# The stick's sums as a rounded part and an exact rest, each multiplied in rounded float32

## The chip, the cores and the metric

The kernel runs on one core of a Trainium2 chip. Its time is device microseconds (us) of one execution. A core has five engines that work beside each other, each through its own queue in order: TensorE (PE: matrix products, with PEld for the loading of its stationary operand), VectorE (DVE), ScalarE (ACT), GpSimd (POOL) and SyncE (SP), which here only issues DMAs. PE writes into PSUM; the other data lies in SBUF.

## The reference, cut to what matters

Two layers over 2048 positions of width 1024. In each layer four groups of heads (A to D) mix the positions, are gated, and go through one output projection. The change lies in group A, stick-breaking attention with 4 heads of 64:

```python
z = einsum('bqhd,bshd->bhqs', qb, kk) * scale
log_1mb = where(strict, log_sigmoid(-z), 0.0)
between = reverse_cumsum(log_1mb) - log_1mb        # sums over later keys
a = where(strict, exp(log_sigmoid(z) + between), 0.0)
y = einsum('bhqs,bshd->bqhd', a, vv)
```

log_sigmoid(-z) is -softplus(z), and log_sigmoid(z) is z - softplus(z). So the exponent of a key is z minus the softplus of this key and of all later ones. That sum over keys is a product with a triangular matrix of minus ones inside a block of 128 keys, and with a full matrix of minus ones for the block after it.

## The kernel before, in words

A layer is a chain of sweeps in the order a, h, d0, d1, b, c, o. Each sweep has 16 steps, one per tile of 128 queries. Sweep a is the one in question: step i projects its tile (`a_prep`), makes the index scores of group C (`ci_prep`, `ci_turn`, `ci_score`), computes the stick's weights (`a_first`, L374) and multiplies them with the values (`a_second`, L425). From tile 4 on, searches for the 256th largest index score (`ci_search`, lines L528 to L656) run beside it: chains of very short DVE instructions on two columns, alternating with counts on ACT.

`a_first` looks at two blocks of keys only, the tile's own and the one before it (one block at i = 0), for 4 heads in two halves r = 0, 1. It goes: scores into the two PSUM tiles `tp` (L391), Abs (L396), Exp (L397) and Ln (L398) on ACT, which leave log(1+exp(-|z|)) in the SBUF tile `x4b`; then DVE adds max(z, 0) (L405), so that `x4b` holds the softplus, called sp here. PE then adds to `tp` the product of sp with `negU`, the triangle of minus ones (L409, 512 columns per half), and of the tile's own block with `nego`, all minus ones (L412, 256 columns per half). Exp (L414) turns `tp` into the weights in `x4c`, which `a_second` multiplies with the values (L436), copies (L440), transposes and writes to DRAM (L445, y<-o).

`negU`, `nego` and sp are float32. The other large products of this kernel (L267, L268, L271, L514, L515) take float32r operands, that is float32 rounded to the shorter form that PE multiplies in one pass, and get their accuracy by splitting a value into a rounded part and the rest (`split`, L199). The rest is made by `psub` (L191) on POOL.

The order of the instructions on each engine comes from two places. `drive` and `merge` weave the generators of a step by the costs that these yield, which sets a priority; a scheduler that simulates the program then orders each engine's queue by readiness and priority. A tile from a pool with `bufs` buffers waits for the last reader of the tile that had the buffer before: `x4b`, `x4c` have one buffer each, `o2` (L174, shown as `o`) has two and also holds `a_second`'s copy and its transposed result until the DMA y<-o has read it.

Of the kernel before, what the change touches and what calls it, by code (L numbers as in the profile page):

```python
# [10 lines left out]
F32 = mybir.dt.float32  # L11
F32R = mybir.dt.float32r
# [77 lines left out]
class Share:  # L90


    def __init__(self, g):
        self.g, self.tot, self.done = g, max(next(g), 1.0), 0.0
# [13 lines left out]
class Trunk:  # L108
    def __init__(self, ctx, tc, I, out, layers=2):
        self.tc, self.nc, self.I, self.out, self.layers = tc, tc.nc, I, out, layers  # L110
        nc = self.nc
        e = ctx.enter_context
        self.dram = e(tc.tile_pool(name="dram", bufs=1, space=DRAM))
        self.cst = e(tc.tile_pool(name="cst", bufs=1))
        self.wk = e(tc.tile_pool(name="wk", bufs=2))
        self.ps = e(tc.tile_pool(name="ps", bufs=2, space=PSUM))
        self.big = e(tc.tile_pool(name="big", bufs=1))
        self.ring = self.big.ring(R1)
        self.rows = self.big.ring(R2)
        dt = self.dram.tile  # L120
        self.hT = [dt([128, 2, KT, 128], F32, name=f"hT{i}") for i in range(NT)]
        self.y = [dt([128, D], F32, name=f"y{i}") for i in range(NT)]
        self.x1 = [dt([128, D], F32, name=f"x1_{i}") for i in range(NT)]
        self.gate = [dt([128, D], F32, name=f"gate{i}") for i in range(NT)]
        self.cT = [dt([128, 3, 128], F32, name=f"cT{i}") for i in range(NT)]
        self.kr = [dt([128, 32], F32, name=f"kr{i}") for i in range(NT)]
        self.sc = [dt([128, 128 * (i + 1)], F32, name=f"sc{i}") for i in range(NT)]
        self.out_of = [dt([128, S], I8, name=f"out_of{i}") for i in range(NT)]
        ct = self.cst.tile
        ld = nc.sync.dma_start  # L130
        self.ident = ct([128, 128], F32, name="ident")
        ld(self.ident, I["c_ident"])
        self.identr = ct([128, 128], F32R, name="identr")
        nc.scalar.copy(self.identr, self.ident)
        self.both = ct([128, 64], F32, name="both")
        self.identb = ct([128, 128], BF, name="identb")
        self.maskA = ct([128, 256], BF, name="maskA")
        self.maskR = ct([128, 512], BF, name="maskR")
        self.negU = ct([128, 128], F32, name="negU")
        self.nego = ct([128, 128], F32, name="nego")  # L140
        nc.gpsimd.memset(self.nego, -1.0)
        self.eps = ct([128, 1], F32, name="eps")
        nc.vector.memset(self.eps, EPS)
        self.mhalf = ct([128, 16], F32, name="mhalf")
        nc.gpsimd.memset(self.mhalf, -0.5)
        self.tie = ct([128, 256], F32, name="tie")
        self.iota9 = ct([128, 9], F32, name="iota9")
        self.junk = ct([128, S], I8, name="junk")
        self.chkA = ct([128, layers], F32, name="chkA")
        self.chkC = ct([128, layers, NT], F32, name="chkC")  # L150
        nc.vector.memset(self.chkC, float(TOPK))
        self.ev = 0

    def constants(self):

        I, ld = self.I, self.nc.sync.dma_start
        ld(self.identb, I["c_identb"])
        ld(self.maskA, I["c_maska"])
        ld(self.negU, I["c_negu"])
        ld(self.tie, I["c_tie"][None, :].to_broadcast([128, 256]))  # L160
        ld(self.iota9, I["c_iota9"])
        ld(self.both, I["c_both"])
        ld(self.maskR, I["c_maskr"])


    def g2(self, shape, dtype=F32):
# [207 lines left out]
    def a_first(self, l, i, st):  # L374
        nc = self.nc
        cur, prev = st["a", i], st.get(("a", i - 1))
        nb = 2 if prev else 1
        n = nb * 256
        yield 1740.0 + 220.0 + 2600.0
        z = [self.psum("tp", (128, 2, 2, 128)) for _ in range(2)]  # L380
        zf = [a.rearrange("p a b c -> p (a b c)") for a in z]
        t = cur[0]
        for r in range(2):
            nc.tensor.matmul(zf[r][:, :256], self.identb, self.maskA, start=True, stop=False, skip_group_check=True)
        yield 220.0
        for b in range(nb):
            kt = (cur, prev)[b][0]
            for p in range(2):
                for r in range(2):
                    q = slice(64 * r, 64 * r + 64)  # L390
                    nc.tensor.matmul(z[r][:, b, p, :], kt[q, 2 + p, :], t[q, p, :],  # L391
                                     start=False, stop=True, skip_group_check=True)
                yield 435.0
        sp = self.x4("b", [128, 2, 512])
        for r in range(2):
            nc.scalar.activation(sp[:, r, :n], zf[r][:, :n], AF.Abs)  # L396
        nc.scalar.activation(sp[:, :, :n], sp[:, :, :n], AF.Exp, scale=-1.0)  # L397
        nc.scalar.activation(sp[:, :, :n], sp[:, :, :n], AF.Ln, bias=1.0)  # L398
        zr = None
        if i >= 2:  # L400
            zr = self.wk.tile([128, 2, 256], F32, name="zr", bufs=1)[0:1]
            for r in range(2):
                nc.vector.tensor_copy(zr[:, r, :], zf[r][0:1, 256:])
        for r in range(2):
            nc.vector.scalar_tensor_tensor(sp[:, r, :n], zf[r][:, :n], 0.0, sp[:, r, :n], op0=OP.max, op1=OP.add)  # L405
        yield 0.0
        pt = self.x4("c", [128, 2, 512])
        for r in range(2):
            nc.tensor.matmul(zf[r][:, :n], self.negU, sp[:, r, :n], start=False, stop=(nb == 1), skip_group_check=True)  # L409
            yield 860.0  # L410
            if nb == 2:
                nc.tensor.matmul(zf[r][:, 256:], self.nego, sp[:, r, :256], start=False, stop=True,  # L412
                                 skip_group_check=True)
            nc.scalar.activation(pt[:, r, :n], zf[r][:, :n], AF.Exp)  # L414
            if zr is not None:

                nc.vector.scalar_tensor_tensor(zr[:, r, :], zr[:, r, :], -1.0, zf[r][0:1, 256:],
                                               op0=OP.mult, op1=OP.add)
            yield 430.0
        if zr is not None:  # L420
            ck = self.chkA[0:1, l:l + 1]
            nc.vector.tensor_scalar(zr, zr, 1.0, None if i == 2 else ck, op0=OP.mult, op1=OP.max, accum_out=ck)
        st["p", i] = pt
# [1049 lines left out]
```

## Time and profile before

| | |
|---|---|
| time, median of 3 runs | 4212.24 us (4211.06 to 4214.72) |
| the profiled execution's own time | 4215.46 us |
| its span, first to last instruction | 4213.2 us |
| PE, DVE, ACT, POOL busy | 93%, 66%, 55%, 32% of the span |
| mean granted clock of PE | 0.961 of full speed |
| sweep a of the two layers | about 12 to 407 us and 2131 to 2530 us |

Busy shares are means over the whole span; a share says what an engine did in a stretch, not who waited for whom. Matmuls overlap, so a matmul's printed duration is longer than the time that it keeps PE from the next one; that time is read from the distance of two starts. A row of the timeline can merge neighbours of one kind (x2: two instructions). One float32 product stands in the trace as two matmul instructions, a float32r product as one.

### The profile page before, as it was taken

How to read it: one execution, taken by the hardware profiler on the slowest of the kernel's cores; microseconds unless marked ns; L12 is line 12 of the kernel's file. 1: busy time of each engine (PE TensorE's matmuls, PEld its weight loads, DVE VectorE, ACT ScalarE, POOL GpSimd, SP SyncE). 2: the span in 40 equal slices, each digit the busy share in tenths (PEclk: the TensorE clock that was granted, in tenths of full speed). 3: DMA queues.
4: the chain of work that ended last, by engine and by line, in shares of the span. 5: the costliest groups of instructions: out<-in, count | busy, mean ns of one | idle time of the engine just before them, and what ended most of it. 6: DMA issues, size and time to landing. Idle time of an engine off the chain costs nothing. (4 is left out here: it accounts for less than half of the span.)

```text
span 4213.2 us, 75287 instructions
## 1 busy us (share of the span) xinstructions
PE 3915.5 (93%) x25833; PEld 3245.7 (77%) x25833; DVE 2787.2 (66%) x10279; ACT 2318.9 (55%) x4797; POOL 1349.2 (32%) x2188
## 2 busy tenths in 40 slices
PE   7999997999978999999999999879899799999998
PEld 7887886878857777777888878768788577777787
DVE  4788677896866655563349995787768666555622
ACT  4566667565655544463245666756656555444621
POOL 2233213455544423210033331224444543232100
PEclk9999997999989999999999999979999899999999
DMA  4223653223200013225522245522232000132244
GB/s 135 103 96 117 198 169 95 80 87 95 86 24 21 18 36 109 73 67 169 170 97 102 90 148 188 165 79 66 79 98 79 27 21 16 48 102 69 64 137 140
DMA packets 227880, 396.49 MB, mean 94 GB/s; under 512 B 66336, under 2 KB 150432, under 8 KB 226976
## 3 DMA queue, kind: packets, MB, share of 16 engines
q1 hardware_dynamic: 227488, 391.59, 29.3%
q8 instruction: 206, 3.38, 0.3%
q14 instruction: 186, 1.52, 0.1%
HBM read 279.00 MB, written 112.49 MB: 93 GB/s over the span
## 5 line engine op out<-in xcount | busy, mean ns | idle before, releaser
L267 PE MATMUL pj<-w_hi,h_hi 128*128 128x384 f32 (+4 forms) x2560 | 870.4, 348 | 39.7 <-ACT w_hi L204 14.1
L268 PE MATMUL pj<-w_lo,h_hi 128*128 128x384 f32 (+4 forms) x2560 | 858.5, 343 | 7.6 <-POOL w_lo L191 5.4
L861 ACT ACTIVATE rw<-rw,at_mn 128x896 f32<-128x896 f32 (+15 forms) x512 | 615.8, 1204 | 200.2 <-DVE at_mn L860 173.7
L296 ACT COPY pt<-tp 128x512 f32<-128x512 f32 (+3 forms) x689 | 356.7, 528 | 426.9 <-PE tp L294 362.8
L294 PE MATMUL tp<-ident,rw 128*128 128x128 f32 x3264 | 543.6, 288 | 50.3 <-DVE rw L1087 32.7
L267 PEld LDWEIGHTS pj<-w_hi,h_hi 128*128 128x128 f32 x2560 | 502.1, 196 | 71.8 <-issue 16.5
L271 PE MATMUL pj<-w_hi,h_lo 128*128 128x384 f32 (+4 forms) x2560 | 529.0, 337 | 0.0
L268 PEld LDWEIGHTS pj<-w_lo,h_hi 128*128 128x128 f32 x2560 | 502.1, 196 | 31.1 <-POOL w_lo L191 7.9
L294 PEld LDWEIGHTS tp<-ident,rw 128*128 128x128 f32 x3264 | 369.6, 144 | 187.1 <-issue 120.2
L857 DVE TENSOR_SCALAR_CACHE_REDUCE rw<-s 128x512 f32<-128x512 f32 x576 | 381.8, 684 | 124.5 <-PE s L851 73.0
L271 PEld LDWEIGHTS pj<-w_hi,h_lo 128*128 128x128 f32 x2560 | 436.0, 191 | 26.6 <-issue 11.8
L282 POOL TENSOR_SCALAR rs<-ss 128x2 f32<-128x2 f32 (+4 forms) x224 | 54.5, 243 | 1039.7 <-DVE ss L925 254.5
L550 ACT ACTIVATE junk<-sg,st_T 128x1152 int8<-128x1152 f32 (+4 forms) x224 | 293.7, 1311 | 72.1 <-DVE st_T L634 52.5
L283 POOL TENSOR_TENSOR rs<-rs,mhalf 128x8 f32<-128x8 f32 (+5 forms) x256 | 310.8, 1215 | 18.6
L298 DVE COPY pt<-tp 128x512 f32<-128x512 f32 (+3 forms) x247 | 153.0, 619 | 194.5 <-PE tp L294 164.8
L851 PE MATMUL s<-dk,qa 96*128 96x512 f32 (+3 forms) x640 | 239.4, 422 | 27.5 <-DVE rw L857 17.0
L197 POOL TENSOR_SCALAR hl<-g 128x256 fp32r<-128x256 f32 (+1 forms) x384 | 144.9, 391 | 360.7 <-DVE g L464 83.5
L851 PE MATMUL s<-bk,qa 128*128 128x512 f32 (+6 forms) x960 | 256.8, 393 | 1.6 <-DVE at_mn L855 1.0
L855 DVE CUSTOM_DVE_ANT_0 rw<-s,maskR 128x128 f32<-128x128 f32 (+3 forms) x400 | 187.4, 478 | 68.0 <-PE s L851 65.9
L294 PE MATMUL pj<-identr,hl 128*128 128x128 f32 (+1 forms) x1280 | 171.1, 256 | 61.4 <-POOL hl L191 36.6
L191 POOL TENSOR_TENSOR hl<-g,hl 128x128 fp32r<-128x128 f32 (+1 forms) x384 | 212.5, 568 | 0.5
L1087 DVE SCALAR_TENSOR_TENSOR rw<-rw,d_c 128x512 f32<-128x512 f32 (+3 forms) x272 | 211.2, 818 | 1.9
(271 smaller groups left out, 8204.3 us busy)
## 6 DMA issues: line engine op xcount, KB each, us to landing
h_hi<-hT SPq DMA_DIRECT2D x128, 512.0 KB, 3.8
h_lo<-hT SPq DMA_DIRECT2D x128, 512.0 KB, 4.9
x4a<-x SPq DMA_DIRECT2D x32, 512.0 KB, 4.8
hT<-h_hi SPq DMA_DIRECT2D x32, 512.0 KB, 2.6
hT<-h_lo SPq DMA_DIRECT2D x32, 512.0 KB, 3.4
x4a<-y SPq DMA_DIRECT2D x32, 512.0 KB, 3.5
x4b<-gate SPq DMA_DIRECT2D x32, 512.0 KB, 3.6
x4c<-x SPq DMA_DIRECT2D x32, 512.0 KB, 4.4
```

What stands on the lines that cost most here:

```text
L191: self.nc.gpsimd.tensor_sub(o, a, b)
L267: nc.tensor.matmul(p[:, :n], hi[:, k, :], whi[k], start=(k == 0), stop=False)
L268: nc.tensor.matmul(p[:, :n], hi[:, k, :], wlo[k], start=False, stop=False)
L271: nc.tensor.matmul(p[:, :n], lo[:, k, :], whi[k], start=False, stop=(k == kt - 1))
L283: nc.gpsimd.tensor_tensor(r, r, self.mhalf[:, :n], op=OP.pow)
L294: nc.tensor.transpose(p[:m, j, :].bitcast(dst.dtype), s.bitcast(dst.dtype), ident)
L296: nc.scalar.copy(dst, p[:m, :len(srcs), :])
L550: nc.scalar.activation(self.junk[:, :ns[g]], Sg[g], AF.Sign, bias=th[:, g:g + 1], scale=-1.0, accum_out=dst[:, g:g + 1])
L851: nc.tensor.matmul(p[:, :w], x, y, start=(k == 0), stop=(k == len(ops) - 1))
L857: nc.vector.tensor_scalar(o, p[:, :w], -scale, None, op0=OP.mult, op1=OP.min, accum_out=m)
L861: nc.scalar.activation(rw, rw, AF.Exp, bias=mn, scale=-1.0, accum_out=ls)
L1087: nc.vector.scalar_tensor_tensor(rows[1][:, c0:e], rows[1][:, c0:e], c, rows[0][:, c0:e], op0=OP.mult, op1=OP.add)
```

## The change

sp is split. `hi` (tile `x4c`) is sp rounded to float32r by two copies on ACT, one per half; `lo` (two tiles from `o2`) is sp - hi by two subtractions on POOL. The two matrices of minus ones are float32r constants now, made at the start through a tile `pt` and a copy on ACT. Both parts meet both matrices: per half and part one product of 512 columns with `negUr` and one of 256 with `negor`. All four subtractions and copies are issued ahead of the products; the weights `pt` take the buffer of `x4c` after hi. The costs that `a_first` yields are new.

```diff
-        self.negU = ct([128, 128], F32, name="negU")
-        self.nego = ct([128, 128], F32, name="nego")
-        nc.gpsimd.memset(self.nego, -1.0)
+        self.negUr = ct([128, 128], F32R, name="negUr")
+        self.negor = ct([128, 128], F32R, name="negor")
+        self.negU, self.nego = self.negUr.bitcast(F32), self.negor.bitcast(F32)
...
+    def rounded_ones(self):
+        nc = self.nc
+        for t, j in ((self.negUr, 0), (self.negor, 1)):
+            f = self.pt([128, 128])
+            if j:
+                nc.gpsimd.memset(f, -1.0)
+            else:
+                nc.sync.dma_start(f, self.I["c_negu"])
+            nc.scalar.copy(t, f)
...
-        yield 1740.0 + 220.0 + 2600.0
+        yield 1740.0 + 220.0 + 1400.0
...
+        hi = self.x4("c", [128, 2, 512], F32R)
+        lo = [self.o2([128, 512], F32R) for _ in range(2)]
+        for r in range(2):
+            nc.scalar.copy(hi[:, r, :n], sp[:, r, :n])
+            self.psub(lo[r][:, :n], sp[:, r, :n], hi[:, r, :n].bitcast(F32))
+        yield 0.0
+        for k, part in enumerate((lambda r: hi[:, r], lambda r: lo[r])):
+            for r in range(2):
+                x = part(r)
+                nc.tensor.matmul(zf[r][:, :n], self.negUr, x[:, :n], start=False, stop=(k == 1 and nb == 1), skip_group_check=True)
+                if nb == 2:
+                    nc.tensor.matmul(zf[r][:, 256:], self.negor, x[:, :256], start=False, stop=(k == 1), skip_group_check=True)
+                yield 345.0
         pt = self.x4("c", [128, 2, 512])
         for r in range(2):
-            nc.tensor.matmul(zf[r][:, :n], self.negU, sp[:, r, :n], start=False, stop=(nb == 1), skip_group_check=True)
-            yield 860.0
-            if nb == 2:
-                nc.tensor.matmul(zf[r][:, 256:], self.nego, sp[:, r, :256], start=False, stop=True,
-                                 skip_group_check=True)
             nc.scalar.activation(pt[:, r, :n], zf[r][:, :n], AF.Exp)
```

The scheduler makes new queues from this. On PE, in step i = 8 of the first layer, before:

```order
L271 MATMUL pj<-w_hi,h_lo 128x384 x4
L409 MATMUL tp<-x4b,negU 128x512
L271 MATMUL pj<-w_hi,h_lo 128x384 x4
L412 MATMUL tp<-x4b,nego 128x256
L409 MATMUL tp<-x4b,negU 128x512
L412 MATMUL tp<-x4b,nego 128x256
L515 MATMUL s<-ik,qb 128x512
```

The same place on PE with the change, where line numbers are those of the changed file (L282 is the old L271, L428 and L430 are the new products, L533 and L534 the old L514 and L515, x4c is hi, and o_2780 is lo of half 0):

```order
L282 MATMUL pj<-w_hi,h_lo 128x384 x8
L428 MATMUL tp<-x4c,negUr 128x512
L430 MATMUL tp<-x4c,negor 128x256
L428 MATMUL tp<-x4c,negUr 128x512
L430 MATMUL tp<-x4c,negor 128x256
L428 MATMUL tp<-o_2780,negUr 128x512
L430 MATMUL tp<-o_2780,negor 128x256
L533 MATMUL s<-ik,qb 128x512
L534 MATMUL s<-ik,qb 128x512
```

The products of hi and those of half 0's rest stand together, right behind one another; four matmuls of the projection that stood between the first two products now stand ahead of them. Half 1's rest (o_2781) comes 31 matmuls after that of half 0, among the transposes of a_prep's queries and keys and ahead of the next step's mask (L395):

```order
L282 MATMUL pj<-w_hi,h_lo 128x384 x8
L305 MATMUL y<-ident,g_2701 128x128 x2
L428 MATMUL tp<-o_2781,negUr 128x512
L305 MATMUL y<-ident,g_2701 128x128
L430 MATMUL tp<-o_2781,negor 128x256
L395 LDWEIGHTS identb
L395 MATMUL tp<-maskA,identb 128x256
```

On POOL in the same step, before (L197 and L191 make a rounded part and a rest: h_hi, h_lo of the next tile, hl of the index vectors; L282 and L283 are the next tile's norm):

```order
L197 TENSOR_SCALAR h_hi<-x4a 128x1024
L507 TENSOR_SCALAR pt<-tie 128x256 x2
L191 TENSOR_TENSOR h_lo<-x4a,h_hi 128x1024
L197 TENSOR_SCALAR hl<-g_2600 128x4x64
L197 TENSOR_SCALAR hl<-g_2600 128x128
L191 TENSOR_TENSOR hl<-g_2600,hl 128x4x64
L191 TENSOR_TENSOR hl<-g_2600,hl 128x128
L282 TENSOR_SCALAR rs<-ss_x 128x1
```

And on POOL with the change, where L208 is the old L197, L202 the old L191 and L526 the old L507:

```order
L208 TENSOR_SCALAR h_hi<-x4a 128x1024
L202 TENSOR_TENSOR h_lo<-x4a,h_hi 128x1024
L202 TENSOR_TENSOR o_2780<-x4b,x4c 128x512
L202 TENSOR_TENSOR o_2781<-x4b,x4c 128x512
L208 TENSOR_SCALAR hl<-g_2690 128x4x64
L208 TENSOR_SCALAR hl<-g_2690 128x128
L202 TENSOR_TENSOR hl<-g_2690,hl 128x4x64
L202 TENSOR_TENSOR hl<-g_2690,hl 128x128
L526 TENSOR_SCALAR pt<-tie 128x256 x2
```

The two new subtractions stand behind h_lo and ahead of the split of the index vectors and the norm.

## Rows read from the trace of the kernel before

**Rows 1.** The page's busy line: us, share of the span, instructions.
```profile
PE 3915.5 (93%) x25833; PEld 3245.7 (77%) x25833; DVE 2787.2 (66%) x10279; ACT 2318.9 (55%) x4797; POOL 1349.2 (32%) x2188
```
**Rows 2.** Windows: stretch, length, busy PE, PEld, DVE, ACT, POOL, clock, DMA, GB/s.
```profile
56.10:118.90 62.80, 61.46 (x408) 55.58 (x406) 24.61 (x53) 26.37 (x56) 19.24 (x26) 1.00 0.26 92
118.90:383.70 264.80, 248.83 (x1538) 216.41 (x1535) 231.34 (x907) 167.28 (x364) 92.75 (x123) 0.97 0.28 99
2198.30:2454.90 256.60, 242.28 (x1539) 211.93 (x1537) 230.19 (x907) 169.21 (x367) 90.27 (x123) 0.99 0.29 101
```
**Rows 3.** One line's instructions, L340 on PE, and its two longest waits (us, times).
```profile
L340 PE MATMUL pj<-ident,x4a x256: 270/273/476, 8.6 to 2457.6; 128*128 128x128 f32 x128
...
  DVE qa L365: 25.3, 22
  DVE x4a L336: 18.0, 4
```
**Rows 4.** One line's instructions, L409 and L412 on PE: min/median/max ns, forms.
```profile
L409 PE MATMUL tp<-x4b,negU x128: 377/592/1061, 50.7 to 2510.0; 128*128 128x512 f32 x120, 128*128 128x256 f32 x8
...
L412 PE MATMUL tp<-x4b,nego x120: 377/379/634, 68.3 to 2510.6; 128*128 128x256 f32 x120
```
**Rows 5.** Timeline of PE, two places: start us, us, engine, line, operation.
```profile
168.34 0.28 PE L515 MATMUL s<-ik,qb 128*128 128x256 f32 x1
168.46 0.28 PE L514 MATMUL s<-ik,qb 128*128 128x256 f32 x1
...
235.63 0.59 PE L412 MATMUL tp<-x4b,nego 128*128 128x256 f32 x2
236.06 1.02 PE L409 MATMUL tp<-x4b,negU 128*128 128x512 f32 x2
236.92 0.59 PE L412 MATMUL tp<-x4b,nego 128*128 128x256 f32 x2
237.17 0.58 PE L515 MATMUL s<-ik,qb 128*128 128x512 f32 x1
237.58 0.39 PE L514 MATMUL s<-ik,qb 128*128 128x512 f32 x1
237.82 0.39 PE L515 MATMUL s<-ik,qb 128*128 128x512 f32 x1
```
**Rows 6.** Groups by form, 0 to 430 us: busy us, mean ns, idle before.
```profile
L296 ACT CAST qb<-pj 128x512 fp32r<-128x512 f32 x16 | 9.3, 583 | 4.0 <-PE pj L294 3.9
...
L191 POOL TENSOR_TENSOR w_lo<-w_raw,w_hi 128x512 fp32r<-128x512 f32 x2 | 2.6, 1290 | 0.1
```
**Rows 7.** Timeline of DVE and PE, two steps: softplus done, first product.
```profile
155.47 1.29 DVE L405 SCALAR_TENSOR_TENSOR x4b<-tp,x4b 128x512 f32<-128x512 f32 x2 [1.72 <-ACT x4b L398]
156.27 1.08 PE L409 MATMUL tp<-x4b,negU 128*128 128x512 f32 x2
...
2506.41 0.67 DVE L405 SCALAR_TENSOR_TENSOR x4b<-tp,x4b 128x512 f32<-128x512 f32 x1
2508.02 1.02 PE L409 MATMUL tp<-x4b,negU 128*128 128x512 f32 x2
```
**Rows 8.** Timeline of POOL, DVE and SP in step i = 8.
```profile
226.34 3.02 POOL L191 TENSOR_TENSOR h_lo<-x4a,h_hi 128x1024 fp32r<-128x1024 f32 x1
226.99 2.39 DVE L618 COPY_PREDICATED st_L<-st_up,st_T 128x4 f32<-128x4 int32 x1
230.97 0.38 SPq L445 DMA_DIRECT2D y<-o  x1
232.39 1.28 DVE L405 SCALAR_TENSOR_TENSOR x4b<-tp,x4b 128x512 f32<-128x512 f32 x2
```
**Rows 9.** Groups by form on DVE, 118.9 to 383.7 us, and one line's durations.
```profile
L615 DVE TENSOR_SCALAR st_nd<-st_T 128x2 f32<-128x2 f32 x21 | 8.8, 417 | 0.0
L613 DVE TENSOR_SCALAR st_up<-st_T 128x2 f32<-128x2 f32 x21 | 7.7, 367 | 0.4
L618 DVE COPY_PREDICATED st_L<-st_up,st_T 128x4 f32<-128x4 int32 x21 | 6.4, 305 | 0.0
...
L618 DVE COPY_PREDICATED st_L<-st_up,st_T x112: 147/156/2386, 141.5 to 2791.7; 128x4 f32<-128x4 int32 x112
```
**Rows 10.** DMA issues, 0 to 430 us: count, KB each, us to landing.
```profile
y<-o SPq DMA_DIRECT2D x14, 128.0 KB, 2.8
```

More of the change, by code (lines that the diff above doesn't have):

```diff
@@ L158, in constants @@
         ld(self.maskA, I["c_maska"])
-        ld(self.negU, I["c_negu"])
+        self.rounded_ones()
         ld(self.tie, I["c_tie"][None, :].to_broadcast([128, 256]))
@@ L418, in a_first @@
                                                op0=OP.mult, op1=OP.add)
-            yield 430.0
         if zr is not None:
```

## The prediction

> **What bounds the kernel now.** I read the page's busy line first: PE is at 93% of the span, DVE at 66%, POOL at 32% [rows 1]. That is a mean over unlike sweeps, so I cut out sweep a, where alone the change works. In its early steps (i = 1 to 3, three steps in 62.8 us) PE is busy 61.46 us and DVE only 24.61: PE alone is the bound. In steps 4 to 13 of the first layer (ten in 264.8 us, 26.5 us each) PE has 248.83 us and DVE 231.34, that is 87%; the second layer reads the same (242.28 and 230.19 of 256.6) [rows 2]. So PE is still the bound there, but with DVE close behind it. The waits say who holds PE when it does stop: its transposes of the next tile (L340) waited 22 times, 25.3 us in all, for DVE's copy L365, which frees a PSUM buffer [rows 3]. Work taken off PE is therefore worth nearly all of itself in the early steps, and less in the later ones.
>
> **What is removed and added on PE.** There are 120 matmuls of 512 columns with the triangle, that is 2 halves x 2 instructions x 30 steps, and 8 of 256 columns (i = 0 of each layer); with the full matrix 120 of 256 columns [rows 4]. What one keeps PE from the next is read from starts: from the first L409 of a pair (236.06) to the L412 behind it (236.92) are 0.86 us for one 512-column product; from L412 (235.63) to L409 (236.06) are 0.43 us for a 256-column one [rows 5]. A half costs 1.29 us, a step 2.58 us. The new products are float32r with a 128x128 stationary operand, like the index scores: 0.24 us from start to start at 512 columns (237.58 to 237.82), 0.12 us at 256 (168.34 to 168.46) [rows 5]. A half now needs two of each, 0.72 us, a step 1.44 us. Saved: 1.14 us in each of 30 steps, 34.2 us; the two steps with one block go from 2 x 0.43 to 4 x 0.12, 0.4 us each. In all 35 us of PE.
>
> **What is added before the products.** Two copies on ACT of 128x512 to float32r: 0.58 us each, as L296's casts of that size; two subtractions on POOL of that size: 1.29 us each, as L191's w_lo [rows 6]. That is 37 us on ACT and 83 us on POOL over 32 steps (the first of each layer at half size); neither is near its limit in sweep a (ACT 167 and POOL 93 of 264.8 us) [rows 2], so what counts is where they delay a waiter.
>
> First the products of hi. They follow the softplus later than before by one copy, and half 1's by two. Before, PE reached the first product with anything from 0.1 to several us to spare. Where it had less than 1.2 us, two copies, I let PE wait for the difference. I read all 30 steps; 10 are so, the first at 156.27 us, where half 0 of L405's pair was done at 156.12, and the last at 2508.02, done at 2507.08 [rows 7]. The differences to 1.2 us sum to about 6 us. Bounds: 0, if the new queue brings PE there later (in step 8 four more projection matmuls stand ahead), and 30 x 1.2 = 36 us, if it is on time everywhere. I take 6.
>
> Then the rest of half 0, which stands on PE right behind hi. It is ready 0.58 + 1.29 = 1.9 us after half 0's softplus. PE finishes hi no sooner than two copies and four products after it, 1.2 + 0.7 = 1.9 us, so this wait is hidden by hi's own, provided POOL is free. h_lo, ahead on POOL, ended at 229.36, the softplus came at 232.39 [rows 8]; I take 0. If POOL came 1 us late in every step it would be 30 us. The rest of half 1 stands 31 matmuls later, at 0.12 to 0.24 us each 4 to 7 us, and is ready 1.3 us after the first: hidden. Behind the subtractions wait the split hl and the next tile's norm on POOL; PE needs both only in the next step, so 2.6 us more there cost nothing.
>
> Next, DVE beside POOL. While POOL ran h_lo (226.34 to 229.36), a DVE instruction of 0.16 us took 2.39 us and ended with it [rows 8]. Three lines of the search show how often: L615, L613 and L618 took 22.9 us for 63 instructions in steps 4 to 13, where 63 x 0.156, L618's median, would be 9.8 [rows 9]. That is 13.1 us lost beside 92.75 us of POOL [rows 2], 0.14 us per us. The subtractions add 2.58 us of POOL per step, so 0.36 us of DVE; over 22 steps with a search about 8 us. Bounds: 0, if they meet only instructions that don't care, and 22 x 2.58 = 57 us, if each stops DVE for its whole length. As DVE is close behind PE there, I count the 8 in full. The Trainium skill, "SBUF — State Buffer", section "Who interferes with whom", speaks against this change: GpSimd and a VectorE instruction that needs the shared port pair exclude each other, and the second waits for the whole of the first. The row of 2.39 us agrees; by that rule at its worst the term is the 57 us.
>
> Last, the shorter PE work meets DVE's pace. In the 22 dense steps part of the 1.14 us only makes L340's wait for L365 longer. None and all of it (25 us) are the bounds; since PE was still busy 94% there, I take a quarter, 6 us.
>
> What else moves: the constants cost two copies on ACT, which its new queue has among the first weights' casts, long ahead of their use: nothing. Outside sweep a the queues keep their order but for small local swaps; I count 0, and 8 us either way in the range.
>
> **Sum.** -35 + 6 + 0 + 8 + 6 = -15 us. The profiled execution took 4215.46 us, of which 4213.2 are its span, and would take 4200; it lies 3.2 us above the median of the three runs, so for the median I say 4197 us. A measurement of this kernel can tell about 0.2% from no change, 8.4 us.
>
> **The rivals.**
> - *Nearly all is kept*: POOL and DVE have air where the subtractions fall, and hi never waits. For it: DVE is idle 13% even in the dense steps [rows 2]. Against it: ten steps without spare time [rows 7]. -35 + 3 = -32, 4180 us.
> - *Swallowed*: PE waits for hi in most steps (some 15 us instead of 6) and DVE's pace takes half of the 25 instead of a quarter; -35 + 15 + 8 + 7 (rounded down, as both waits can be one) = -5, 4207 us, no change to be told. For it: the dense steps are bound by both engines [rows 2].
> - *Slower, by POOL stopping DVE*: the two subtractions run back to back just when the search's chain of short instructions runs, and each holds DVE for its length. Price up to 57 us; with the 6 for hi it turns the gain into a loss once more than 29 of them, half, reach PE. For it: 2.39 us in place of 0.16 [rows 8]. Against: over all of POOL's work the share was 0.14, not 0.5 [rows 9]. At three quarters, 43: -35 + 6 + 43 = +14, 4226 us.
> - *Slower, by the rest's buffers*: lo of half 1 takes a buffer that the DMA y<-o must have read. In step 8 that DMA was issued at 230.97 [rows 8] and lands 2.8 us later [rows 10], at 233.8; the subtraction would start at 232.39 + 0.64 + 0.58 + 1.29 = 234.9. Only 1.1 us to spare for POOL, though 4 more for PE. SP's queue holds y<-o behind other DMAs that wait for POOL and DVE; 2 us of wait on PE in each step would cost 60: -35 + 60 = +25, 4237 us.
> - *It doesn't do what it says*: a float32r product with this operand costs what float32 does. Then PE has 30 x 2.58 = 77 us more, 4289 us. The index scores speak clearly against it [rows 5].
>
> **How the numbers follow.** Forecast 0.47, with 4188 to 4203 as its own range; nearly all kept 0.15; swallowed 0.20; POOL stopping DVE 0.11; buffers 0.05; no saving 0.02. Faster by over 0.2% is below 4203.8: the forecast and the first rival, 0.61 with their edges. Within: swallowed and a little of the forecast's edge, 0.21. Slower: the last three, 0.18. For 8 in 10 the range runs from 4178 (below nearly all kept) to 4224 (short of the slower cases' middle).
>
> **What would show it.** Right: in the profile after, the new products stand 0.24 and 0.12 us apart; steps of sweep a are shorter, by about 1 us at i = 1 to 3 and by less later; DVE's busy share in steps 4 to 13 rises above 90%, and L340's wait for L365 grows; PE's waits for `x4c` (hi) sum to under 10 us and those for lo to nearly nothing. Wrong: sweep a not shorter, with PE waiting for lo or for the split on POOL, or with the search's short instructions stretched far more than now; or a change of more than 8 us outside sweep a. The clock matters little as long as its mean there stays at 0.97 to 1.00 [rows 2].

## The result, and the profile after

The change makes the kernel slower: 4253.71 us (median of 5 runs, 4250.45 to 4255.97) against 4212.24 us for the kernel before, measured with it, a ratio of 1.0094 with a 95% interval of [1.0082, 1.0107]. That is +41 us where -15 was forecast, and outside the range. One run of a kernel below (costs of 2400) took 5690.55 us at a granted clock of 0.599; it is left out of that kernel's ratio.

The page's busy line after, which answers [rows 1]:

```profile
PE 3885.6 (91%) x25833; PEld 3233.7 (76%) x25833; DVE 2822.8 (66%) x10279; ACT 2355.5 (55%) x4863; POOL 1433.0 (34%) x2252
```

POOL has 84 us more and ACT 37, as worked out ahead (83 and 37). PE has less. DVE has as many instructions as before, and is busy 36 us longer with them. That is the first sign.

The timeline of PE after, in step 8 (start us, us, engine, line), answers [rows 5]: L428 and L430 are the new products, x4c is hi, o is lo.

```profile
240.95 0.39 PE L428 MATMUL tp<-x4c,negUr 128*128 128x512 f32 x1
241.18 0.28 PE L430 MATMUL tp<-x4c,negor 128*128 128x256 f32 x1
241.30 0.39 PE L428 MATMUL tp<-x4c,negUr 128*128 128x512 f32 x1
...
241.65 0.39 PE L428 MATMUL tp<-o,negUr 128*128 128x512 f32 x1
```

From start to start a product of 512 columns keeps PE 0.23 us (240.95 to 241.18) and one of 256 columns 0.12. The PE work saved is as forecast. The windows after, steps 1 to 3 and 4 to 13 of layer 0 (stretch, length, busy PE, PEld, DVE, ACT, POOL, clock, DMA, GB/s), answer [rows 2]:

```profile
55.00:114.90 59.90, 58.25 (x408) 54.52 (x406) 25.18 (x52) 30.05 (x62) 28.78 (x34) 1.00 0.28 97
114.90:378.60 263.70, 237.79 (x1517) 214.08 (x1516) 228.09 (x815) 164.00 (x359) 112.48 (x137) 0.95 0.28 99
```

The early steps took 59.9 us instead of 62.8, 1 us less each. The dense steps took 263.7 us instead of 264.8: PE is busy 11 us less, and the stretch is as long as it was. DVE got through 815 instructions instead of 907: its searches and scores have fallen behind. The granted clock fell from 0.97 to 0.95. Of PE's waits in these steps the one for DVE's copy `o`, which `a_second` makes, grew most. Before and after (us, times, longest):

```profile
PE y L294 <- DVE o L440: 0.4, 1, 0.4
```

```profile
PE y L305 <- DVE o L459: 5.5, 3, 4.0
```

To see where the lost time shows, I cut each layer at three events: the end of sweep a on PE (the last L436), the first product of sweep d0, and the end of the searches, that is of their rounds (the last L634, L653 after). The last searches of a layer still run on DVE beside the start of d0, which needs DVE for its own work; what they find is read only after sweep b has begun (first at 1245 us, L945). The windows of before, layer 0, cut there, and the last one up to the first product of sweep b:

```profile
0.00:459.00 459.00, 411.72 (x2485) 358.10 (x2486) 334.61 (x1197) 257.12 (x556) 150.07 (x206) 0.97 0.36 117
459.00:644.00 185.00, 175.14 (x838) 154.31 (x838) 129.80 (x717) 131.13 (x265) 36.39 (x64) 0.95 0.60 185
644.00:724.00 80.00, 60.41 (x346) 54.98 (x345) 63.10 (x423) 67.60 (x129) 24.99 (x46) 0.81 0.27 82
724.00:1215.00 491.00, 456.81 (x3405) 390.13 (x3403) 399.16 (x1345) 300.30 (x667) 236.55 (x389) 0.95 0.26 79
```

And after, cut at the same events:

```profile
0.00:464.00 464.00, 402.51 (x2492) 359.65 (x2493) 342.19 (x1175) 267.03 (x576) 181.95 (x231) 0.96 0.35 115
464.00:647.00 183.00, 169.85 (x830) 148.64 (x829) 128.07 (x639) 121.71 (x262) 44.64 (x71) 0.97 0.60 191
647.00:746.00 99.00, 68.53 (x401) 62.20 (x400) 75.74 (x530) 86.62 (x152) 30.07 (x54) 0.80 0.25 79
746.00:1244.00 498.00, 454.33 (x3341) 383.06 (x3341) 396.38 (x1337) 298.43 (x661) 227.49 (x378) 0.94 0.25 75
```

The first row of each says that sweep a did not become shorter: its last product came at 459 us before (later than the 407 of the table ahead) and at 464 after, and in layer 1, counted from the layer's first product (at 2090 and 2114 us), at 444 and 456.

Now the third row: between d0's first product and the end of the searches PE is busy only 60 of 80 us, at a mean granted clock of 0.81, so in part at the lower level of 1.2 GHz. This stretch grew from 80 to 99 us. The searches ended at 724 us and now at 746, and sweep b came 29 us later. In layer 1 the searches ended at 708 and now at 734, and b came 12 us later. Sweeps b to o of both layers took 6 us less, so that the two profiled executions, of 4213.2 and 4248.6 us from first to last instruction, differ by 35 us.

DVE's busy time up to the end of the searches, the sum of the first three rows, is 334.61 + 129.80 + 63.10 = 527.5 us before and 546.0 after, for 2337 and 2344 instructions. Layer 1 gives 520.8 and 540.8. Together DVE lost 38.5 us on work that did not change.

What took them is seen in the timeline after, at 263 us (start us, us, engine, line). The first row stands for the two new subtractions, one behind the other:

```profile
263.07 2.60 POOL L202 TENSOR_TENSOR o<-x4b,x4c 128x512 fp32r<-128x512 f32 x2 [4.06 <-ACT x4c L422]
263.14 1.29 DVE L635 TENSOR_TENSOR st_nd<-st_nd 128x2 f32<-128x2 f32 x1
264.43 1.25 DVE L647 TENSOR_TENSOR st_md<-st_L,st_H 128x2 f32<-128x2 f32 x1
```

L635 and L647 work on two columns and otherwise take 0.15 us; here the first lasted until the first subtraction ended, and the second until the second did. I counted in the records, up to the end of the searches in both layers, the DVE instructions that lie more than 0.3 us above the median of their own line, tiles and shape: 78 with 72 us too much before, 119 with 115 us after. Each of them overlaps an instruction of POOL. In 33, with 34 us of the 115, the end falls within 0.1 us of the end of a new subtraction. A few instructions are held; the rest run as fast as they did.

### The profile page after: what moved, and what is told of

Same layout as the page of the kernel before. It is cut to its first block, busy times and chain, and to the rows that moved or that the text cites. A ratio compares the mean times of both kernels' runs of the same rounds, so it can differ in the third digit from the quotient of the medians.

```text
span 4248.6 us, 75422 instructions
## 1 busy us (share of the span) xinstructions
PE 3885.6 (91%) x25833; PEld 3233.7 (76%) x25833; DVE 2822.8 (66%) x10279; ACT 2355.5 (55%) x4863; POOL 1433.0 (34%) x2252
## 5 line engine op out<-in xcount | busy, mean ns | idle before, releaser
L880 ACT ACTIVATE rw<-rw,at_mn 128x896 f32<-128x896 f32 (+15 forms) x512 | 615.7, 1205 | 168.2 <-DVE at_mn L879 147.2
L282 PE MATMUL pj<-w_hi,h_lo 128*128 128x384 f32 (+4 forms) x2560 | 526.1, 335 | 0.0
L282 PEld LDWEIGHTS pj<-w_hi,h_lo 128*128 128x128 f32 x2560 | 435.5, 190 | 19.7 <-issue 4.2
L874 DVE CUSTOM_DVE_ANT_0 rw<-s,maskR 128x128 f32<-128x128 f32 (+3 forms) x400 | 187.5, 478 | 62.0 <-PE s L870 59.9
L536 ACT ACTIVATE pt<-s 128x512 f32<-128x512 f32 (+3 forms) x304 | 158.4, 545 | 110.5 <-PE s L534 46.1
L899 PE MATMUL y<-pt,dv 128*64 128x128 f32 x2176 | 190.8, 303 | 30.9 <-DVE o L1129 19.6
L208 POOL TENSOR_SCALAR hl<-g 128x256 fp32r<-128x256 f32 (+1 forms) x384 | 143.3, 387 | 218.6 <-DVE g L483 48.4
```

Of the source, the lines that this page charges most:

```text
L282: nc.tensor.matmul(p[:, :n], lo[:, k, :], whi[k], start=False, stop=(k == kt - 1))
L874: nc.vector.tensor_tensor_reduce(o, p[:, :w], b, -scale, 3.0e38, OP.add, OP.min, m)
L880: nc.scalar.activation(rw, rw, AF.Exp, bias=mn, scale=-1.0, accum_out=ls)
L899: nc.tensor.matmul(y[o:o + 64, :], v(j), pt[:, c * m:(c + 1) * m, :].rearrange("p a b -> p (a b)"), start=(j < 2), stop=(j >= nb - 2), ski ...
```

## The experiments

The question was where 41 us come from. In the expectations, O stands for the new order of the queues, Q for POOL's queue behind the subtractions, B for the shared buffers; D says that DVE's work up to the end of the searches sets the time, P that PE's does, W that the change's own waits lose the time, V that the order set by the costs does, S that the index scores and searches decide when the sweeps after a get through. Each ratio is to the kernel before, run on the same chip.

**Without the rest.** The products of lo and the subtractions are left out, so the sums are only the rounded ones.

```diff
-            self.psub(lo[r][:, :n], sp[:, r, :n], hi[:, r, :n].bitcast(F32))
-        for k, part in enumerate((lambda r: hi[:, r], lambda r: lo[r])):
+        for k, part in enumerate((lambda r: hi[:, r],)):
```

> The changed kernel without the rest: no subtractions, and only the products of hi, so the weights are those of a rounded softplus. Theory Q (the subtractions stand at the head of POOL's queue waiting for hi, hold up the split of the index vectors and the score's ties behind them, so index scores and searches end late): the delay is gone, 4165 to 4195 us. Theory B (lo takes o2's buffers, so PE must transpose a_second's result early and stands waiting for DVE's copy): gone too, 4165 to 4195. Theory O (the new costs and instructions only make the scheduler weave the step differently, scores and searches later): still slow, 4225 to 4260.

Measured 4231.14 us, 1.0054 [1.0037, 1.0071]. Sweep a ended 28 and 18 us earlier than before, and the kernel is still slower: the searches ended at 733 (724 before) and at 723 of layer 1 (708). So neither POOL's queue nor the buffers can be all of it.

**The subtractions on DVE.**

```diff
-            self.psub(lo[r][:, :n], sp[:, r, :n], hi[:, r, :n].bitcast(F32))
+            self.nc.vector.tensor_sub(lo[r][:, :n], sp[:, r, :n], hi[:, r, :n].bitcast(F32))
```

> The changed kernel with the two subtractions on DVE in place of POOL, lo still in o2's buffers. Theory Q: POOL's queue is free again, the index scores come on time, but DVE itself now waits for hi; 4195 to 4225 us, and POOL's wait for hi is gone. Theory B: PE still stands waiting for DVE's copy o, 4235 to 4265. Theory O: no statement beyond a different order, 4200 to 4260.

Measured 4262.58 us, 1.0130 [1.0107, 1.0152]. POOL is free of them and as few DVE instructions are held as before (77 with 74 us by the count above), but DVE has 64 more to do and is busy as long as in the changed kernel (2825.1 and 2822.8 us), and the searches ended at 754 and 742. That is no better than having them on POOL.

**The costs alone, in the kernel before.**

```diff
-        yield 1740.0 + 220.0 + 2600.0
+        yield 1740.0 + 220.0 + 1400.0
-            yield 860.0
+            yield 460.0
-            yield 430.0
+            yield 230.0
```

> The kernel before with nothing changed but the costs that a_first yields, set to the sum of the new ones (1400 in place of 2600). Theory O: this alone brings a good part of the loss, 4225 to 4255 us. Theories Q and B: no change beyond the noise of another order, 4200 to 4222.

Measured 4232.98 us, 1.0064 [1.0044, 1.0084]: the same instructions in another order, 27 us slower, with DVE's busy time as it was (2787.2 us).

**The old costs in the changed kernel** (2600 instead of 1400, 645 instead of 345).

> The changed kernel with the old sum of costs (2600, spread over the four groups of products). Theory O: most of the loss goes, 4190 to 4220 us. Theories Q and B: still slow, 4235 to 4265, with POOL waiting for hi and PE for the copy o as in the changed kernel.

Measured 4228.12 us, 1.0053 [1.0033, 1.0073]; the searches ended at 733 and 723. That lies between what O and what Q and B expected: some 19 of the 41 us come with the new costs, 22 with the change itself.

**Searches of three rounds instead of eight**, before and after. The general path is left out too, so the searches are shorter and the selection coarser.

```diff
-NITER = 8
+NITER = 3
```

> The kernel before with 3 in place of 8 rounds of every search and without the general path behind the flag; the searches end unfinished. Theory S (index scores and searches are the chain that decides when sweeps h, d0 and d1 get through; sweep a's PE work is beside it): 7 searches of 5 rounds less at 4 to 9 us a round in each layer, of which a third to a half shows, so 4020 to 4130 us. Theory W (PE itself decides, and the new waits of the changed stick make sweep a longer): little, 4180 to 4212.

> The changed kernel with the same 3 rounds of search and no general path. Theory S: with the searches short, the PE work that the change saves shows, 15 to 45 us below the kernel before with short searches. Theory W: still slower than that one by 15 to 45 us.

Measured 4132.18 us, 0.9820 [0.9803, 0.9836], and 4120.01 us, 0.9788 [0.9771, 0.9804]. With short searches the change is 12 us faster, close to the -15 of the forecast and less than the 15 to 45 that S expected. The searches then end at 603 us (before) and 588 (after), ahead of d0's first product (642 and 633). The sign of the change hangs on the searches.

**Scores and searches first**, before and after.

```diff
-LATER = {"search": -30, ...
+LATER = {"search": -300, ...
-                gs.append(self.ci_score(l, i, st))
+                gs.append(self.at(-100, self.ci_score(l, i, st)))
```

> The kernel before with the searches and index scores put further ahead in the scheduler's priority (300 for 30 and 100 for 0). Theory S: the searches end earlier in both layers, 4170 to 4212 us. Theory W: later work of sweep a only gives way, 4205 to 4240.

> The changed kernel with the same priorities. Theory S: the scores and searches no longer come late, so it loses most of what it lost and is at or below the kernel before with these priorities: 4160 to 4212 us. Theory W: 4240 to 4270, above that kernel by 25 us or more.

Measured 4223.01 us, 1.0033 [1.0023, 1.0043], and 4248.74 us, 1.0097 [1.0080, 1.0113]. The searches of before end earlier (706 and 698), but sweep a is 18 and 35 us longer: DVE is needed by both, and order only moves the loss. The changed kernel gains nothing and stays 26 us above the other. Here S failed, and the times are those that W expected.

**Slightly lower costs in the kernel before** (2400, 800 and 400).

> The kernel before with the costs that a_first yields lowered a little (2400 in place of 2600), nothing else. Theory O (any new weaving of sweep a loses, as the old one was better than its neighbours): 4220 to 4250 us. Otherwise, if 2600 to 1400 mattered by its size: 4200 to 4216.

Measured 4213.55 us, 1.0000 [0.9986, 1.0014]. Not every new order loses: the 27 us above are the price of one order, and don't say what that of the changed kernel costs.

**Two tiles of its own for the rest.**

```diff
-        lo = [self.o2([128, 512], F32R) for _ in range(2)]
+        lo = [self.wk.tile([128, 512], F32R, name="lo", bufs=2) for _ in range(2)]
-R2 = 30720
+R2 = 28608
```

> The changed kernel with two buffers of its own for the rest, so that o2 is left to a_second as before (the ring of rows is 2112 bytes smaller for it). Theory B (sharing o2 makes PE wait for DVE's copy of a_second): PE's wait for the copy o goes, sweep a is 5 to 15 us shorter per layer, 4220 to 4240 us in all, as far as the searches let it through. Theory S (the searches decide): 4230 to 4260, with the time reappearing at the start of d0.

Measured 4312.92 us, 1.0233 [1.0209, 1.0258]. To make room I had cut a ring of buffers of other sweeps by 2112 bytes. After it the searches of tiles 8 to 11 ended their first round at 577 us, 32 us after the last score (3 us after it in the changed kernel), so the smaller ring may have held them up, and the comparison is spoiled. It tells nothing of the buffers; a later run does.

**One pair's search started earlier**, before and after.

```diff
- ("h", 3): ((12, 13), (14, 15))}
+ ("h", 1): ((12, 13),), ("h", 3): ((14, 15),)}
```

> The kernel before with the search of tiles 12 and 13 issued at step 1 of sweep h, not at step 3 beside that of 14 and 15. Theory S: the searches end 10 to 30 us earlier in each layer and d0's start is shorter by a part, 4160 to 4205 us. Theory W (PE work and waits of sweep a decide): no change, 4200 to 4220.

> The changed kernel with the search of tiles 12 and 13 issued at step 1 of sweep h. Theory S: 20 to 50 us below the changed kernel, 4200 to 4235, and nearer to the kernel before with the same edit than the 41 us now. Theory W: 4240 to 4260.

Measured 4215.30 us, 1.0008 [0.9995, 1.0022], and 4274.51 us, 1.0144 [1.0121, 1.0167]. The searches of before then ended at 841 us instead of 724, at the same time of the kernel; those of the changed kernel ended at 871, and it lost 59 us to its twin. S failed here too, as it expected a gain of both. So nothing waits for their end as such: it marks how far DVE has come, and only for kernels with the same groups of searches.

**Less work for DVE**, before and after: the check of the weights (L403, L417, L422) and the general path behind it are left out. PE's products stay.

```diff
-        if i >= 2:
+        if i >= 99:
...
-        Trunk(ctx, tc, I, out, inputs["w_in"].shape[0]).all()
+        Trunk(ctx, tc, I, out, inputs["w_in"].shape[0]).all(False)
```

> The kernel before without the check of the weights (the DVE reductions at L403 and L417, the sums behind them and the general path are left out; the PE products are all there). About 67 us of DVE work goes, most of it in the 30 steps. Theory D (in sweep a the searches and scores on DVE, not the products on PE, set when d can begin): the end of the last search round moves some 20 us forward in each layer and the time falls to 4150 to 4195. Theory P (PE sets the pace in sweep a): the time stays within 10 us of 4210.

> The changed kernel with the same DVE work left out. Theory D: with room on DVE the shorter products count, so the gap of 41 us between the two kernels closes to 15 or less, or turns to a gain of up to 30. Theory W (the new waits: POOL's queue held by subtractions that wait for hi, and the shared o buffers): the gap stays at 30 to 50, since none of them needs DVE's reductions.

Measured 4195.44 us, 0.9968 [0.9955, 0.9982], and 4204.42 us, 0.9987 [0.9976, 0.9998]. The gap is 9 us instead of 41. The time of before fell less than D expected (14 us; 4150 to 4195 was said), and its searches ended 14 us earlier in the first layer but 5 us later in the second (713, 708 with the check). The windows up to the end of the searches, the kernel before without that work:

```profile
0.00:461.00 461.00, 416.34 (x2503) 360.67 (x2504) 320.67 (x1139) 263.25 (x569) 148.02 (x212) 0.97 0.35 118
461.00:639.00 178.00, 170.61 (x821) 150.34 (x821) 126.84 (x761) 135.25 (x266) 32.49 (x58) 0.96 0.58 190
639.00:709.00 70.00, 56.26 (x336) 49.60 (x334) 56.34 (x357) 55.88 (x115) 25.04 (x46) 0.86 0.29 94
```

and the changed kernel without it:

```profile
0.00:469.00 469.00, 413.14 (x2538) 364.78 (x2538) 342.86 (x1138) 279.77 (x603) 188.16 (x244) 0.96 0.35 117
469.00:640.00 171.00, 163.61 (x788) 142.86 (x786) 122.03 (x728) 129.47 (x259) 33.19 (x58) 0.97 0.61 195
640.00:711.00 71.00, 54.68 (x324) 49.43 (x323) 57.37 (x384) 61.01 (x120) 21.71 (x42) 0.83 0.26 82
```

DVE still loses 18 us to the change (503.9 and 522.3 us), but now it has room: the searches end at 709 and 711, in layer 1 at 713 and 707. W fails on this pair, since the new waits are all still there.

**The same with two tiles of its own for the rest**, the ring R1 64 bytes smaller.

> As e14, and the rest lies in two tiles of its own instead of two of the four buffers that the transposed rows use. Theory W in its part on the buffers: 10 to 20 us below e14. Theory D: within 8 us of e14.

Measured 4202.87 us, 0.9983 [0.9971, 0.9995], 1.5 us from its twin. Sweep a ended 14 us earlier in the first layer and 17 in the second than in that twin, and yet the time is the same: the shared buffers lengthen sweep a and cost the kernel nothing here.

**More work for PE**, in the kernel before: its result is then another, as the sums count twice.

```diff
+            nc.tensor.matmul(zf[r][:, :n], self.negU, sp[:, r, :n], start=False, stop=False, skip_group_check=True)
             nc.tensor.matmul(zf[r][:, :n], self.negU, sp[:, r, :n], start=False, stop=(nb == 1), skip_group_check=True)
```

> The kernel before with the product with the matrix of minus ones made twice in each half (its result is then another; the second adds two fp32 products of up to 512 columns to a step, 1.7 us at full width, 51 us over 30 steps, on PE alone). Theory P: 40 to 55 us slower than before. Theory D: 0 to 25 us slower, since PE then fills time in which it waits for DVE in the same sweep.

Measured 4231.45 us, 1.0047 [1.0030, 1.0065], 20 us for some 51 us of PE. The windows:

```profile
0.00:478.00 478.00, 433.65 (x2569) 365.38 (x2569) 347.43 (x1225) 263.00 (x570) 153.32 (x212) 0.99 0.34 114
478.00:655.00 177.00, 169.54 (x820) 148.87 (x816) 128.22 (x777) 137.53 (x267) 32.89 (x58) 0.96 0.59 192
655.00:713.00 58.00, 42.66 (x252) 38.27 (x250) 49.36 (x317) 49.12 (x100) 18.44 (x36) 0.84 0.28 89
```

Sweep a became 19 us longer and the third stretch 22 us shorter; the searches ended at 713 instead of 724. In layer 1 they ended later, at 727 instead of 708, and sweep b came 12 us later. Of 51 us more of PE 20 show: in this run more than half of it is cover, and not path.

**The two halves of the change, each alone.** First the shorter products alone: the functions write sp rounded (the exact rest is left out), the matrices are rounded, and there is no cast, subtraction or new cost.

```diff
-        sp = self.x4("b", [128, 2, 512])
+        spr = self.x4("b", [128, 2, 512], F32R)
+        sp = spr.bitcast(F32)
...
-            nc.tensor.matmul(zf[r][:, :n], self.negU, sp[:, r, :n], start=False, stop=(nb == 1), skip_group_check=True)
+            nc.tensor.matmul(zf[r][:, :n], self.negUr, spr[:, r, :n], start=False, stop=(nb == 1), skip_group_check=True)
```

> The kernel before, in which the functions write the sums as rounded values themselves (the exact rest is left out, so the sums carry the rounding) and the four products a step are rounded ones. No cast, no subtraction, no new wait, the old costs: only PE's work is shorter, 1.86 us a step at full width, 56 us over 30 steps. Theory D: the end of the searches stays where it was within 10 us and the time is 0 to 20 us below before. Theory W (the change loses by its own waits and added work, and PE's time counts): 35 to 55 us below before.

Measured 4226.62 us, 1.0043 [1.0026, 1.0060]: 18 us slower, outside what either theory expected. The windows:

```profile
0.00:427.00 427.00, 373.12 (x2396) 335.63 (x2397) 310.19 (x1141) 246.80 (x539) 137.07 (x197) 0.97 0.37 123
427.00:616.00 189.00, 179.98 (x868) 158.07 (x867) 129.57 (x625) 114.10 (x255) 40.19 (x73) 0.96 0.58 186
616.00:732.00 116.00, 75.79 (x443) 69.00 (x442) 89.45 (x592) 99.00 (x167) 29.72 (x56) 0.80 0.26 82
732.00:1228.00 496.00, 450.51 (x3302) 379.39 (x3302) 394.87 (x1324) 297.01 (x657) 232.31 (x379) 0.93 0.24 73
```

This is the clearest reading of the case. Sweep a is 32 us shorter, as much as PE saved there (28 us by the starts, half of the 56), and d0 starts 28 us earlier. But DVE has the same 529 us of work (527.5 before), so more of it is left when d0 starts: the searches end at 732, and the third stretch is 36 us longer. PE waits in it for DVE, as its waits from 616 to 732 us show (us, times, longest):

```profile
PE s L862 <- DVE at_mn L866: 12.5, 3, 11.8
PE tp L304 <- DVE rw L1098: 6.2, 3, 5.3
PE pj L304 <- POOL hl L201: 5.9, 4, 2.6
PE y L891 <- DVE o L1121: 5.8, 2, 4.9
```

The longest of these waits, 11.8 us up to 729 us, was for L866, d0's own work on its scores. Of these 11.8 us DVE ran instructions of the search for 10.6. Three of them, and L866 behind them:

```profile
719.46 1.95 DVE L653 TENSOR_SCALAR_CACHE_REDUCE ge<-sg,st_T 128x1664 int8<-128x1664 f32 x1
...
723.62 1.89 DVE L656 MAX8 st_ex<-sg 128x8 f32<-128x1664 f32 x1
...
726.13 1.94 DVE L663 SCALAR_TENSOR_TENSOR ge<-sg,st_sp,ge 128x1664 int8<-128x1664 f32 x1
...
728.27 0.69 DVE L866 CUSTOM_DVE_ANT_0 rw<-s,maskR 128x512 f32<-128x512 f32 x1
```

In the changed kernel PE's longest wait in the third stretch, 8.4 us up to 743 us, is put down to POOL's `hl`; for 7.9 of them DVE was in the search as well.

Then the additions alone: the cast and the subtractions beside the old products, read by nobody.

```diff
+        hi = self.x4("c", [128, 2, 512], F32R)
+        lo = [self.o2([128, 512], F32R) for _ in range(2)]
+        for r in range(2):
+            nc.scalar.copy(hi[:, r, :n], sp[:, r, :n])
+            self.psub(lo[r][:, :n], sp[:, r, :n], hi[:, r, :n].bitcast(F32))
         pt = self.x4("c", [128, 2, 512])
```

> The kernel before, and beside it the cast to hi on ACT and the two subtractions on POOL in each step, into the same tiles as in the change, with nobody reading them; the products stay in fp32. No PE work is saved and no product waits for the cast. Theory D with the additions as the load that reaches DVE: 20 to 45 us slower than before, DVE's busy time up by some 30 us. Theory V (the loss lies in the order that the new costs set): within 10 us of before.

Measured 4241.45 us, 1.0078 [1.0059, 1.0098], 33 us. The windows, and one row of POOL's waits from 114 to 420 us:

```profile
0.00:473.00 473.00, 418.25 (x2491) 361.26 (x2492) 352.74 (x1197) 271.63 (x585) 185.76 (x237) 0.96 0.35 113
473.00:652.00 179.00, 174.06 (x837) 152.06 (x836) 125.39 (x684) 127.22 (x262) 36.85 (x66) 0.97 0.60 194
652.00:740.00 88.00, 65.59 (x391) 60.10 (x391) 68.32 (x463) 74.99 (x139) 28.89 (x54) 0.83 0.28 89
```

```profile
POOL o L191 <- ACT x4c L410: 49.3, 9, 8.7
```

DVE's busy time up to the end of the searches is 546.5 us, 19 more than before, as in the changed kernel (546.0), and the searches end at 740. In this kernel 123 DVE instructions are held, with 115 us too much; with the products alone it was 74 with 71. So the stalls come with the additions, and not with the shorter products. Sweep a is 14 us longer here, and 17 in layer 1.

What stays open. The halves cost 18 and 33 us, together with the old costs 22, with the new ones 41: they don't add. A new order of the same instructions cost between 0 and 27 us, so of the 18 us of the products alone I can't say how much is its order and how much that PE reaches d0 early and waits there at the lower clock. That shorter products alone gain little is shown: with 56 us less of PE the kernel is 18 us slower, and no new order of the same instructions cost more than 27. That they lose by themselves is not shown. Nor is it shown how much of the 41 us is the 38.5 us that DVE lost; that the two figures are close proves nothing. The costs alone lost 27 us with no DVE time lost, and the pair without the check lost 9 us with 47 us more of DVE (2738.6 and 2785.6 us on their pages).

## Why the prediction was wrong, point by point

*What bounds the kernel now.* This is where it failed. The view was right and too narrow: in sweep a PE is at 94% and DVE at 87%, and I took the busier engine for the bound. I never looked at what DVE still owes when the sweep ends. The third row of the windows cut at the searches' end would have shown it in the trace of before: PE at 60 of 80 us and clock 0.81, with DVE's searches still running. A shorter sweep a only starts this wait sooner, as the products alone show. In the changed kernel sweep a did not even become shorter (464 and 456 us for 459 and 444).

*Removed and added on PE, -35.* The work was right (0.23 and 0.12 us, 1 us less in each of steps 1 to 3). Its worth was not: the products alone took 54 us off sweep a in the two layers (459 to 427, 444 to 422) and gave all of it back behind it. "Outside sweep a ... I count 0" and "a quarter, 6 us" for DVE's pace are the terms that fell. The signs named for that quarter did not come either: in steps 4 to 13 DVE is busy 228.09 of 263.7 us, 86% and not above 90%, and the transposes' wait for the copy that frees their PSUM buffer (L351 for L376 now) fell from 25.3 to 22.2 us. PE stood for DVE's copy `o` instead, and behind the sweep.

*hi +6, the rest 0.* PE's line L428 waited 1.8 us in all for hi, 6 times; for lo it shows no wait. Both terms were small, as said. (The sums of added work were taken over 32 full steps; with the first of each layer at half size, as the text there has it, they are 36 and 80 us, where 37 and 84 were measured.) The row of L428 in the profile after:

```profile
  ACT x4c L422: 1.8, 6
```

*POOL's queue behind the subtractions, 0.* Not nothing on POOL itself. Its wait after, from 115 to 420 us:

```profile
POOL o L202 <- ACT x4c L422: 64.1, 11, 8.6
```

The subtractions stand at the head of POOL's queue and wait for hi, up to 8.6 us, and all that is behind them waits too. PE's waits don't name it, and the kernel without subtractions lost 23 us without it. What it costs was not separated from the rest of the additions.

*DVE beside POOL, +8.* The mechanism was right and the size was off: 38.5 us of DVE, 0.46 us per added us of POOL (84 us) instead of 0.14. I had taken the rate from three lines of the search and divided by all of POOL's work, though other DVE lines are held as well: all of them had 72 us too much before, up to the end of the searches. After the change the same three lines in steps 4 to 13, which answer [rows 9], were held less than before (mean ns 367, 417 and 305 then, in this order):

```profile
L632 DVE TENSOR_SCALAR st_up<-st_T 128x2 f32<-128x2 f32 x17 | 5.4, 319 | 0.3
L634 DVE TENSOR_SCALAR st_nd<-st_T 128x2 f32<-128x2 f32 x17 | 4.3, 253 | 0.0
L637 DVE COPY_PREDICATED st_L<-st_up,st_T 128x4 f32<-128x4 int32 x17 | 4.2, 248 | 0.0
```

Others took the blow. Up to the end of the searches of layer 0 the line that squares st_nd had 170 ns on average:

```profile
L616 DVE TENSOR_TENSOR st_nd<-st_nd 128x2 f32<-128x2 f32 x56 | 9.5, 170 | 0.0
```

and after the change 210:

```profile
L635 DVE TENSOR_TENSOR st_nd<-st_nd 128x2 f32<-128x2 f32 x56 | 11.8, 210 | 0.0
```

The rule of the Trainium skill, "SBUF — State Buffer", section "Who interferes with whom", which had spoken against the change, agrees with the 1.29 us of L635 beside the subtraction; the 38.5 us lie below its worst case of 57.

*The rivals.* "Slower, by POOL stopping DVE" came closest: it put 43 us on DVE, and 38.5 were measured. It ended at 4226 us because it kept the 35 us of PE as a gain. The rest's buffers fell with the tiles of its own (1.5 us of the time, though 14 and 17 of sweep a). That a float32r product costs as much as a float32 one fell with the rows of PE.

*The costs.* That the new costs by themselves are worth 19 to 27 us was in no term. I had read the order only for where single instructions stand.

*The clock.* It was to matter little as long as its mean in these steps stayed at 0.97 to 1.00. In steps 4 to 13 it was 0.95; what that cost was not measured apart.

## What to carry to other kernels

Ask of a busy engine what the others still owe when its stretch ends: cut the trace where one stage's work runs on into the next, here at the start of d0 and the end of the searches, and see which engine the next stage waits for there. An engine at 94% beside one at 87% can be cover; take away work of each alone, as here with the products alone and the additions alone, before the sum is believed. Work that is put on POOL can cost DVE too, here 38.5 us for 84; look which of the two engines is late before PE's saving is counted as a gain.

## What the runs showed of the hardware that was not expected

DVE's work was slowed by POOL's at a rate of nearly one half: 84 us of 128x512 subtractions on POOL (mean 1.39 us each in sweep a of layer 0) cost 38.5 us of DVE, by some 40 more instructions that are held, those beside a subtraction up to 1.3 us. The same subtractions on DVE itself cost it as much (38 us over the whole trace, where POOL's cost 36). Where PE waits for DVE and POOL at the start of d0, its granted clock is 0.80 to 0.86 in the windows shown, against 0.93 to 0.99 in the stretches around it. In the kernel before the products of L880 took 372 ns in the median there and 273 in sweeps d0 and d1 behind it (724 to 1215 us): part of what the wait costs is paid in slower products.
